# A gated convolution's result stored as two rounded parts, and loaded without a split ahead of its projection

## The chip, the core and the metric

The kernel runs on 1 core of one Trainium2 chip. The metric is device time in microseconds (us) of one execution. Three executions of the kernel before gave 1155.13 us (median), from 1154.42 to 1155.83.

Engines are named as in the profile: PE (TensorE matmuls; PEld its weight loads), DVE (VectorE), ACT (ScalarE), POOL (GpSimd), SP (SyncE, which here only issues DMAs; ACT issues some too).

## The reference, cut to what matters

An encoder layer over a sequence of 1024 rows and 1024 features, with two branches that read the same normalised input. One branch is a gated long convolution of width 512 ("hyena"), the other is attention with 8 heads. The change touches the result of the convolution, `zc` times its gate, between the convolution and the matmul with `w_hy_out`.

```python
h = rms_norm(x, g_norm[l])
proj = h @ w_in[l]
hy_in, z_hy, c_q, c_kv, k_rope, z_attn, gate_hy, gate_attn = jnp.split(proj, split_at, axis=-1)
u = short_conv(hy_in, w_short[l], b_short[l])
v_h, x1, x2 = jnp.split(u, 3, axis=-1)
zc = v_h
for o, gate in enumerate((x1, x2)):
    zc = gate * long_conv(zc, k_spec[:, o], hy_bias[l, o])
u_hy = (zc * jax.nn.silu(z_hy)) @ w_hy_out[l]
...
attn = dense_bidirectional_attention(q, k, v_a)
u_attn = (attn * jax.nn.silu(z_attn)) @ w_attn_out[l]
merged = g_hy * u_hy + g_at * u_attn
x = x + merged @ w_out[l]
```

## The kernel before, in words

Every f32 operand of a matmul is written as a sum of two rounded parts, high and low (type fp32r, names ending in h and l), and each product is made of three matmuls: high by high, high by low, low by high (`mm3`, L119, L121, L122). The helper `split` makes the parts: ACT casts the high part (L138), and DVE, or POOL where it is named, subtracts it for the low part (L139).

The stages in order of time. First the normalised input and the convolution's filters. Then the convolution in two halves, `convs(0)` and `convs(1)`, of two blocks of 128 features each (b = 0, 1 and b = 2, 3). Then `qkv`, which makes queries, keys and values (`pq`, `pkr`) and stores them to DRAM. Then what is left of the projections `pm` (L567) of the input onto the gate columns; these matmuls need nothing of the convolution and are strewn as filler between the stages from the filter on. Then attention: per head `pth` transposes queries and keys (L857), `S` holds the scores, `pr` the exponentials, `pt` their transposes (L901), `pv` the product with the values. Last comes the rest of the convolution branch, the projection of the attention branch, and the product with `w_out`.

**The result of the convolution.** At the end of `convs`, for each block b, a gate tile `gt` of 128x1024 is loaded from DRAM (L711), multiplied by the transposed convolution `pty` (L716, DVE), and stored to `yT[b]` in DRAM (L718). `gt` comes from a pool with one buffer, so the load for the next block waits until the tile of the block before is free.

**Its way back.** `hyena_load` (L986) loads the four `yT[b]` into tiles `yr` (L991) from a tag "gg" with three buffers, and splits each into `yh[i]` on ACT and `yl[i]` on POOL. `branch_out` (L963) then takes, for each of eight blocks d of the output columns, 256 KB of `w_hy_out` into a tile `wr` (L971), splits it into `wh` and `wl` (POOL while attention runs, DVE behind it), loads a gate tile `gg` (L976), and runs 24 matmuls `pmo` with the four `yh[i]` and `yl[i]`. Blocks d = 0, 1, 2 are written inside the pools of attention, as filler for PE; blocks 3 to 7 come behind attention.

**What sets the order.** The program text does not fix each engine's order. When the program is built, a list scheduler places all instructions on the engines by what is ready, and each engine then runs its list strictly in order. DMAs of SP are issued in the order of SP's list, onto one queue (q1); those of ACT onto another (q10). Near the start of attention, the queues' lists hold: the loads `qr`, `kr`, `vr` of the first pair of heads (L834), the `yr` loads, the `wr` loads of `w_hy_out`, the `gg` loads, and loads `z` (L935) for the attention's own gate. ACT's list holds there the casts `yh` and `wh`, and the pairs `ob` (L683), which read the projections `pm` out of PSUM; `pth` writes to PSUM space that the last `ob` has read.

Of the kernel before, what the change touches and what calls it, by code (L numbers as in the profile page):

```python
# [10 lines left out]
F32 = mybir.dt.float32  # L11
F32R = mybir.dt.float32r
# [7 lines left out]
P = 128  # L20
L = 1024
# [72 lines left out]
class K:  # L94
# [529 lines left out]
    def scratch(self):  # L624
        nc, a = self.nc, self.a
        dp = self.dp
        self.yT = [dp.tile([P, L], F32, tag=f"yT{i}", name=f"yT{i}") for i in range(4)]
        self.cT = [dp.tile([P, L], F32, tag=f"cT{i}", name=f"cT{i}") for i in range(6)]
        self.zaT = [dp.tile([P, L], F32, tag=f"zaT{i}", name=f"zaT{i}") for i in range(4)]
        self.gT = [dp.tile([P, L], F32, tag=f"gT{i}", name=f"gT{i}") for i in range(16)]  # L630
        self.g2, self.ud, self.xd = {}, {}, {}
# [61 lines left out]
    def convs(self, hf):  # L693
        nc = self.nc
        NB = CW // P
        uy = lambda nme: self.uq.tile([P, 8, CW], F32, tag="UY", bufs=2, name=self.nm(nme))
        U = uy("U")
        for g in range(2):
            nc.sync.dma_start(out=U[:, 4 * g:4 * g + 4], in_=self.ud[hf][g])
        Y = self.conv(0, hf, U)  # L700
        for g in range(2):
            xt = self.uq.tile([P, 4, CW], F32, tag="xt", name=self.nm("xt"))
            nc.sync.dma_start(out=xt, in_=self.xd[hf][g])
            nc.vector.tensor_tensor(out=Y[:, 4 * g:4 * g + 4], in0=Y[:, 4 * g:4 * g + 4], in1=xt, op=ALU.mult)
        for i in range(NB):
            self.xz(hf * NB + i)
        Y = self.conv(1, hf, Y)
        for i in range(NB):
            b = hf * NB + i
            gt = self.uq.tile([P, L], F32, tag="xt", name=self.nm("gt"))  # L710
            nc.sync.dma_start(out=gt, in_=self.g2[b])  # L711
            for g in range(2):
                ps = self.pp.tile([P, 4, P], F32, tag="cv", bufs=CVB, name=self.nm("pty"))
                for j in range(4):
                    nc.tensor.transpose(out=ps[:, j], in_=Y[:, 4 * g + j, i * P:(i + 1) * P], identity=self.ident)
                nc.vector.tensor_tensor(out=gt[:, g * 512:(g + 1) * 512], in0=gt[:, g * 512:(g + 1) * 512],  # L716
                                        in1=ps.rearrange("p a b -> p (a b)"), op=ALU.mult)
            nc.sync.dma_start(out=self.yT[b], in_=gt)  # L718


    def qkv(self, kp):
# [115 lines left out]
    def attention(self, wp, ssp, sp):  # L837

        nc, a = self.nc, self.a
# [111 lines left out]
        for u in range(64):  # L951
            h, qb = divmod(u, 8)
            if u + 1 < 64:
                scores(u + 1)
            trans(u)
            if u + 1 < 64:
                soft(u + 1)
            if u >= 2:
                pvs(u // 2 - 1, u % 2)
            if h + 1 < H and 2 <= qb < 6:  # L960
                prep(h + 1, qb - 2)
        pvs(31, 0)
# [19 lines left out]
                nc.vector.tensor_tensor(out=g[:, sl], in0=g[:, sl], in1=ps, op=ALU.mult)  # L982
                done(d, c, g[:, sl])

    def hyena_load(self, tp):
        nc = self.nc  # L986
        self.yh = [tp.tile([P, L], F32R, tag=f"yh{i}", name=f"yh{i}") for i in range(4)]
        self.yl = [tp.tile([P, L], F32R, tag=f"yl{i}", name=f"yl{i}") for i in range(4)]
        for i in range(4):
            y = tp.tile([P, L], F32, tag="gg", bufs=3, name=self.nm("yr"))  # L990
            nc.sync.dma_start(out=y, in_=self.yT[i])  # L991
            self.split(y, self.yh[i], self.yl[i], nc.gpsimd)
        self.m1 = {(d, c): self.dp.tile([P, 512], F32, tag=f"m1_{d}_{c}", name=f"m1_{d}_{c}") for d in range(8) for c in range(2)}

    def hyena_out(self, tp, pp, ds):
        def done(d, c, x):
# [155 lines left out]
@with_exitstack  # L1152
def hyena_mla_kernel(ctx, tc, a, out):
    k = K(ctx, tc, a, out)
    k.cp = ctx.enter_context(k.pool("cp"))
    k.dp = ctx.enter_context(k.pool("dp", space=DRAM))
    k.scratch()
    with k.pool("pp", space=PSUM) as k.pp:
        with ExitStack() as sr:
            hp = sr.enter_context(k.pool("hp", side="right"))  # L1160
            k.wp = sr.enter_context(k.pool("wp", side="right"))
            k.op = sr.enter_context(k.pool("op", side="right"))
            with k.pool("fp") as fp:
                with k.pool("xp") as xp, k.pool("fp1") as f1:
                    k.setup(xp)
                    k.load_x(xp, 0)
                    k.load_x(xp, 1)
                    k.filter_loads(f1)
                    k.build_hT(hp, xp)
                    k.filter_mlp(fp, f1)  # L1170
                    k.selection()
                svw = ExitStack()
                k.vw = svw.enter_context(k.pool("vw", side="right"))
                with k.pool("fpb") as fb:
                    k.filter_tables(fb)
                    with k.pool("fwk") as wk:
                        k.filter_spectra(wk)
                        for b in range(GEARLY):
                            k.fill_g(b)
            with k.pool("uq") as k.uq, k.pool("gp") as gp, k.pool("vb") as k.vb:  # L1180
                k.proj_vx(0)
                k.load_gu(gp)
                k.convs(0)
                k.proj_vx(1)
                k.convs(1)
            svw.close()
            for b in range(6):
                k.fill_c(b)
            with k.pool("kp") as kp:
                k.qkv(kp)  # L1190
            yp = ctx.enter_context(k.pool("yp"))
            srp = ExitStack()
            k.rp = srp.enter_context(k.pool("rp"))
            k.raw = {}
            k.load_pair(0)
            for b in range(4):
                k.fill_z(b)
            for b in range(GEARLY, 16):
                k.fill_g(b)
            k.hyena_load(yp)  # L1200
    with k.pool("gp2", side="right") as g2:
        k.ah = [g2.tile([P, L], F32R, tag=f"ah{i}", name=f"ah{i}") for i in range(4)]
        k.al = [g2.tile([P, L], F32R, tag=f"al{i}", name=f"al{i}") for i in range(4)]
        with k.pool("ssp", space=PSUM) as ssp, k.pool("asp", space=PSUM) as sp, k.pool("awp") as wp:
            k.mb = 1
            k.attention(wp, ssp, sp)
            k.hyena_out(yp, sp, range(HSPLIT))
        srp.close()
        with k.pool("tps", space=PSUM) as pp, k.pool("tlp") as tp:
            k.mb = 8  # L1210
            k.hyena_out(yp, pp, range(HSPLIT, 8))
            k.tail(yp, g2, tp, pp)
# [39 lines left out]
```

## Time and profile before

| | us |
|---|---|
| median of 3 executions | 1155.13 |
| lowest, highest | 1154.42, 1155.83 |
| the profiled execution | 1159.08 |
| its span in the profile | 1156.9 |
| PE busy | 1098.8 (95%) |
| DVE busy | 894.0 (77%) |
| ACT busy | 589.2 (51%) |
| POOL busy | 106.7 (9%) |

The profiled execution is one more execution than the three of the median, with its own time. The span is what the trace covers of it; the rest, 2.2 us, lies around it. Times of single instructions, as in the rows below, count from the start of the span. "Busy" adds up the time in which an engine executes something. The mean granted clock of PE was 0.984 of full speed.

### The profile page before, as it was taken

What the parts mean: (1) busy time and instruction counts of PE and PEld (TensorE: products, weight loads), DVE (VectorE), ACT (ScalarE), POOL (GpSimd) and SP (SyncE); (2) the same over time, 40 slices, a digit from 0 to 9 for tenths busy, and PEclk for the clock granted to TensorE, in tenths of its full rate; (3) what the DMA queues carried; (4) which work ended last, traced back from release to release, by engine and by line L of the source; (5) the groups of instructions that cost most, each with busy time, mean ns of one, the idle gap of its engine ahead of it and who ended that gap; (6) DMA issues with size and microseconds to landing.
All of it is one profiled execution on the core that took longest, in us unless ns stands there. A gap on an engine that the chain in (4) does not pass through costs nothing.

```text
span 1156.9 us, 15518 instructions
## 1 busy us (share of the span) xinstructions
PE 1098.8 (95%) x5525; PEld 912.7 (79%) x5525; DVE 894.0 (77%) x1631; ACT 589.2 (51%) x1097; POOL 106.7 (9%) x108
## 2 busy tenths in 40 slices
PE   4899999999999999999998999799999999999996
PEld 3678888888888888878887887688888888777875
DVE  6988788698788886778774793488888888678872
ACT  5735655754445434434424752687777777321420
POOL 0000000000000000000000132400000000232253
PEclk9989999999999999999999999899999999999999
DMA  5446454642335334334327558610202010886345
GB/s 211 132 146 194 153 166 175 204 119 64 88 90 142 110 110 131 91 90 125 91 82 226 153 152 284 201 56 12 90 1 92 1 65 1 265 272 208 90 129 182
DMA packets 119221, 150.27 MB, mean 130 GB/s; under 512 B 8548, under 2 KB 82408, under 8 KB 119144
## 3 DMA queue, kind: packets, MB, share of 16 engines
q1 hardware_dynamic: 107688, 120.97, 34.4%
q10 hardware_dynamic: 11456, 28.32, 6.5%
q8 instruction: 43, 0.70, 0.3%
q14 instruction: 34, 0.28, 0.1%
HBM read 101.81 MB, written 47.45 MB: 129 GB/s over the span
## 4 chain that ended last, share of the span: by engine, by line
PE 77%; DVE 8%; DMA 8%; ACT 4%; issue 2%; POOL 1%; SPq 0%; POOLq 0%; ACTq 0%; DVEq 0%
PE pm L567 35%; PE pu L128 8%; PE pt L901 5%; PE pi L128 4%; PE S L119 2%; PE S L121 2%; PE S L122 2%; PE pv L913 2%; PE pv L914 2%; PE po L122 2%; PE po L121 2%; PE po L119 2%; PE pmo L121 1%; PE pmo L119 1%; ACT pr L888 1%
## 5 line engine op out<-in xcount | busy, mean ns | idle before, releaser
L567 PE MATMUL pm<-hh,wh 128*128 128x512 f32 x656 | 208.8, 394 | 1.4 <-DVE hl L143 0.5
L567 PE MATMUL pm<-hl,wh 128*128 128x512 f32 x656 | 209.4, 394 | 0.0
L567 PE MATMUL pm<-hh,wl 128*128 128x512 f32 x656 | 208.3, 392 | 0.1
L567 PEld LDWEIGHTS pm<-hh,wh 128*128 128x128 f32 x656 | 123.1, 189 | 27.3 <-ACT wh L138 0.7
L567 PEld LDWEIGHTS pm<-hh,wl 128*128 128x128 f32 x656 | 123.4, 189 | 26.0 <-DVE wl L139 0.5
L567 PEld LDWEIGHTS pm<-hl,wh 128*128 128x128 f32 x656 | 123.5, 189 | 25.4
L138 ACT CAST wh<-wr 128x512 fp32r<-128x512 f32 x98 | 60.3, 621 | 152.0 <-PE pm L567 106.9
L138 ACT CAST PTh<-pt 128x512 fp32r<-128x512 f32 x128 | 72.8, 587 | 43.6 <-PE pt L901 41.8
L139 DVE TENSOR_TENSOR PTl<-pt,PTh 128x512 fp32r<-128x512 f32 x128 | 84.0, 683 | 14.0 <-ACT PTh L138 13.7
L886 DVE TENSOR_REDUCE mx<-S 128x1 f32<-128x1024 f32 x64 | 77.8, 1218 | 10.5 <-PE S L122 10.1
L139 DVE TENSOR_TENSOR wl<-wr,wh 128x512 fp32r<-128x512 f32 x95 | 66.2, 702 | 16.2 <-ACT wh L138 16.1
L901 PE MATMUL pt<-ident,pr 128*128 128x128 f32 x512 | 75.1, 276 | 1.1 <-ACT pr L888 0.2
L888 ACT ACTIVATE pr<-S,mx 128x1024 f32<-128x1024 f32 x64 | 71.7, 1121 | 5.4 <-DVE mx L886 5.1
L901 PEld LDWEIGHTS pt<-ident,pr 128*128 128x128 f32 x512 | 59.1, 140 | 15.5 <-ACT pr L888 2.9
L913 PE MATMUL pv<-PTh,vc 128*128 128x256 f32 x256 | 68.9, 297 | 0.0
L914 PE MATMUL pv<-PTl,vc 128*128 128x256 f32 x256 | 67.8, 293 | 0.0
L473 DVE TENSOR_TENSOR t<-pu,kt 128x512 f32<-128x512 f32 x64 | 41.0, 681 | 31.2 <-PE pu L128 30.5
L138 ACT CAST rh<-res 128x512 fp32r<-128x512 f32 x64 | 39.5, 619 | 42.8 <-PE pu L128 20.2
L119 PE MATMUL S<-kh,qh 96*128 96x512 f32 x128 | 53.0, 414 | 1.7 <-ACT pr L888 1.6
L121 PE MATMUL S<-kh,ql 96*128 96x512 f32 x128 | 52.5, 410 | 0.0
L913 PEld LDWEIGHTS pv<-PTh,vc 128*128 128x128 f32 x256 | 48.5, 189 | 4.4 <-DVE at L924 1.6
L122 PE MATMUL S<-kl,qh 96*128 96x512 f32 x128 | 50.8, 398 | 0.0
(285 smaller groups left out, 2402.2 us busy)
## 6 DMA issues: line engine op xcount, KB each, us to landing
wr<-in_w_in_dram SPq DMA_DIRECT2D x82, 256.0 KB, 3.2
wor<-in_w_out_dram SPq DMA_DIRECT2D x36, 256.0 KB, 4.6
dec<-in_dec_dram SPq DMA_DIRECT2D x16, 512.0 KB, 3.7
gT<-ob ACTq DMA_DIRECT2D x16, 512.0 KB, 3.3
gg<-gT SPq DMA_DIRECT2D x16, 512.0 KB, 3.9
kd<-kt ACTq DMA_DIRECT2D x28, 256.0 KB, 2.2
kt<-kd SPq DMA_DIRECT2D x28, 256.0 KB, 2.7
m<-gg ACTq DMA_DIRECT2D x16, 256.0 KB, 3.5
```

The lines of the kernel that those rows point to most:

```text
L119: m = nc.tensor.matmul(out, lhsT=lh, rhs=rh, start=start, stop=False)
L121: nc.tensor.matmul(out, lhsT=ll, rhs=rh, start=False, stop=False)
L122: nc.tensor.matmul(out, lhsT=lh, rhs=rl, start=False, stop=stop)
L128: m = self.nc.tensor.matmul(out, lhsT=x, rhs=y, start=n == 0, stop=n == len(ops) - 1)
L138: self.behind(self.nc.scalar.copy(out=hi, in_=x), after)
L139: (eng or self.nc.vector).tensor_tensor(out=lo, in0=x, in1=hi.bitcast(F32), op=ALU.subtract)
L567: nc.tensor.matmul(ps[c][0:m], lhsT=w[:, i, 0:m], rhs=h[d][:, c * 512:(c + 1) * 512], start=(d == 0 and f == 0), stop=(d == 7 and f == 2))
L886: nc.vector.tensor_reduce(out=mx, in_=ps, axis=AX.X, op=ALU.max, negate=True)
L888: nc.scalar.activation(out=pr, in_=ps, func=AF.Exp, bias=mx, accum_out=RS[h // 2][:, qb, h % 2:h % 2 + 1])
L901: nc.tensor.transpose(out=pt[:, i], in_=pr[:, kb * P:(kb + 1) * P], identity=self.ident)
L913: nc.tensor.matmul(pv, lhsT=V[h][:, kb], rhs=hi[:, kb], start=(kb == 0), stop=False)
L914: nc.tensor.matmul(pv, lhsT=V[h][:, kb], rhs=lo[:, kb], start=False, stop=(kb == 7))
```

## The change

`convs` splits each finished block into a high and a low part there, on ACT and DVE, and stores both: `yT[b]` becomes a pair of DRAM tiles. `hyena_load(i)` now loads block i's two parts from DRAM straight into `yh[i]` and `yl[i]`; the tiles `yr`, the four casts on ACT and the four subtracts on POOL are gone from that place. In the text of the program the call stands inside the loop of attention, at steps u = 8, 12, 16 and 20 of 64, and `hyena_tiles` only sets the tiles up.

```diff
@@ -624,7 +624,7 @@
     def scratch(self):
         nc, a = self.nc, self.a
         dp = self.dp
-        self.yT = [dp.tile([P, L], F32, tag=f"yT{i}", name=f"yT{i}") for i in range(4)]
+        self.yT = [[dp.tile([P, L], F32, tag=f"yT{x}{i}", name=f"yT{x}{i}") for x in "hl"] for i in range(4)]
         self.cT = [dp.tile([P, L], F32, tag=f"cT{i}", name=f"cT{i}") for i in range(6)]
         self.zaT = [dp.tile([P, L], F32, tag=f"zaT{i}", name=f"zaT{i}") for i in range(4)]
         self.gT = [dp.tile([P, L], F32, tag=f"gT{i}", name=f"gT{i}") for i in range(16)]
@@ -715,7 +715,10 @@
                     nc.tensor.transpose(out=ps[:, j], in_=Y[:, 4 * g + j, i * P:(i + 1) * P], identity=self.ident)
                 nc.vector.tensor_tensor(out=gt[:, g * 512:(g + 1) * 512], in0=gt[:, g * 512:(g + 1) * 512],
                                         in1=ps.rearrange("p a b -> p (a b)"), op=ALU.mult)
-            nc.sync.dma_start(out=self.yT[b], in_=gt)
+            y = [self.uq.tile([P, L], F32R, tag=f"y{x}", name=self.nm("y" + x)) for x in "hl"]
+            self.split(gt, *y)
+            for x in range(2):
+                nc.sync.dma_start(out=self.yT[b][x], in_=y[x].bitcast(F32))
 
 
     def qkv(self, kp):
@@ -957,6 +960,8 @@
                 soft(u + 1)
             if u >= 2:
                 pvs(u // 2 - 1, u % 2)
+            if u % 4 == 0 and 8 <= u < 24:
+                self.hyena_load(u // 4 - 2)
             if h + 1 < H and 2 <= qb < 6:
                 prep(h + 1, qb - 2)
         pvs(31, 0)
@@ -982,15 +987,14 @@
                 nc.vector.tensor_tensor(out=g[:, sl], in0=g[:, sl], in1=ps, op=ALU.mult)
                 done(d, c, g[:, sl])
 
-    def hyena_load(self, tp):
-        nc = self.nc
+    def hyena_tiles(self, tp):
         self.yh = [tp.tile([P, L], F32R, tag=f"yh{i}", name=f"yh{i}") for i in range(4)]
         self.yl = [tp.tile([P, L], F32R, tag=f"yl{i}", name=f"yl{i}") for i in range(4)]
-        for i in range(4):
-            y = tp.tile([P, L], F32, tag="gg", bufs=3, name=self.nm("yr"))
-            nc.sync.dma_start(out=y, in_=self.yT[i])
-            self.split(y, self.yh[i], self.yl[i], nc.gpsimd)
         self.m1 = {(d, c): self.dp.tile([P, 512], F32, tag=f"m1_{d}_{c}", name=f"m1_{d}_{c}") for d in range(8) for c in range(2)}
+
+    def hyena_load(self, i):
+        for x, t in enumerate((self.yh, self.yl)):
+            self.nc.sync.dma_start(out=t[i].bitcast(F32), in_=self.yT[i][x])
 
     def hyena_out(self, tp, pp, ds):
         def done(d, c, x):
@@ -1197,7 +1201,7 @@
                 k.fill_z(b)
             for b in range(GEARLY, 16):
                 k.fill_g(b)
-            k.hyena_load(yp)
+            k.hyena_tiles(yp)
     with k.pool("gp2", side="right") as g2:
         k.ah = [g2.tile([P, L], F32R, tag=f"ah{i}", name=f"ah{i}") for i in range(4)]
         k.al = [g2.tile([P, L], F32R, tag=f"al{i}", name=f"al{i}") for i in range(4)]
```

Since the scheduler sets each engine's order, three places show what moved. Line numbers behind the change are by 3 to 6 higher for the same statement. In the rows, x<-y is what is written and read.

SP's issues at the end of the convolution, between block b = 2 and the first loads of `wst` (weights of `qkv`), before:

```order
L718 DMA yT_62<-gt_5074 128x1024
L559 DMA wr_6996<-in_w_in_dram 128x4x128
L711 DMA gt_5089<-g_3_4660 128x1024
L718 DMA yT_63<-gt_5089 128x1024
L559 DMA wr_7032<-in_w_in_dram 128x4x128
L735 DMA wst_5522<-in_w_uq_dram 128x768
```

and with the change:

```order
L721 DMA yTh_64<-yh_5102 128x1024
L721 DMA yTl_65<-yl_5103 128x1024
L711 DMA gt_5108<-g_3_4674 128x1024
L559 DMA wr_7056<-in_w_in_dram 128x4x128
L721 DMA yTh_66<-yh_5122 128x1024
L721 DMA yTl_67<-yl_5123 128x1024
L559 DMA wr_7086<-in_w_in_dram 128x4x128
L738 DMA wst_5546<-in_w_uq_dram 128x768
```

Each block now has two stores in place of one, and the weight loads `wst` stand behind the second store of the last block, which is issued when DVE has made the low part.

SP's issues at the start of attention, before (three `yr` loads stand in a row, and two `wr` loads):

```order
L834 DMA qr_6356<-qd 128x1536
L834 DMA kr_6357<-kdr 128x1536
L834 DMA vr_6358<-vd 128x1024
L991 DMA yr_7170<-yT_60 128x1024
...
L971 DMA wr_9970<-in_w_hy_out_dram 128x4x128
...
L991 DMA yr_7182<-yT_63 128x1024
L976 DMA gg_9976<-gT_74 128x1024
```

and with the change:

```order
L837 DMA qr_6380<-qd 128x1536
L837 DMA kr_6381<-kdr 128x1536
L837 DMA vr_6382<-vd 128x1024
L997 DMA yh_7186<-yTh_60 128x1024
L997 DMA yl_7190<-yTl_61 128x1024
...
L997 DMA yh_7189<-yTh_66 128x1024
L997 DMA yl_7193<-yTl_67 128x1024
L938 DMA z_7998<-zaT_74 128x512
...
L976 DMA wr_9986<-in_w_hy_out_dram 128x4x128
...
L981 DMA gg_9992<-gT_78 128x1024
```

All eight loads of `yh` and `yl` stand in a row directly behind `vr`, not among the steps of attention; the first `wr` of `w_hy_out` stands behind them and behind two `z` loads.

ACT and PE at the start of attention. ACT before (the casts of `yr`, three and one, stand ahead of the last `ob` pair):

```order
L138 CAST yh_7162<-yr_7170 128x1024
...
L138 CAST yh_7164<-yr_7178 128x1024
L138 CAST wh_9972<-wr_9970 128x512
...
L138 CAST yh_7165<-yr_7182 128x1024
L683 ACTIVATE ob_7158<-pm_7096,cols 128x512
...
L684 DMA gT_89<-ob_7158 128x1024
...
L142 ACTIVATE qh_7228<-pth_7230,gq 96x512
...
L142 ACTIVATE kh_7244<-pth_7246,cols 96x512
...
L888 ACTIVATE pr_7273,rs_7270<-S_7263,mx_7271 128x1024
```

and with the change:

```order
L683 ACTIVATE ob_7182<-pm_7120,cols 128x512
...
L684 DMA gT_93<-ob_7182 128x1024
L142 ACTIVATE qh_7236<-pth_7238,gq 96x512
...
L142 ACTIVATE kh_7252<-pth_7254,cols 96x512
...
L138 CAST wh_9988<-wr_9986 128x512
...
L891 ACTIVATE pr_7281,rs_7278<-S_7271,mx_7279 128x1024
```

The last `ob` pair has no cast of a `yr` ahead of it, and the first `wh` stands behind `qh` and `kh`. PE's list at the same place, before (rows that continue a pattern left out):

```order
L567 MATMUL pm_7097<-hh_146,wl_7131 128x512
L857 MATMUL pth_7230<-ident,qr_6356 96x128 x4
L857 MATMUL pth_7237<-ident,qr_6356 96x128 x4
L119 MATMUL pmo_9978<-yh_7162,wh_9972 128x512
L121 MATMUL pmo_9978<-yh_7162,wl_9973 128x512
...
L857 MATMUL pth_7246<-ident,kr_6357 96x128 x4
...
L119 MATMUL S_7263<-kh_7244,qh_7228 128x512
```

and with the change:

```order
L567 MATMUL pm_7121<-hh_150,wl_7155 128x512
L860 MATMUL pth_7238<-ident,qr_6380 96x128 x4
L860 MATMUL pth_7245<-ident,qr_6380 96x128 x4
L860 MATMUL pth_7254<-ident,kr_6381 96x128 x4
...
L119 MATMUL S_7271<-kh_7252,qh_7236 128x512
...
L119 MATMUL pmo_9994<-yh_7186,wh_9988 128x512
L121 MATMUL pmo_9994<-yh_7186,wl_9989 128x512
```

Before, 28 `pmo` matmuls stand ahead of the first `pt` of attention, the first of them ahead of the transposes of `kr`. With the change 12 do, all in a row behind the scores `S`, and the `pt` stand behind them. Of the 192 matmuls `pmo` that read `yh` and `yl`, 120 stand behind attention before, and 156 with the change.

## Rows read from the trace of the kernel before

**Rows 1.** Three windows: PE, PEld, DVE, ACT, POOL busy us (instructions), PEclk, DMA share, GB/s

```profile
720.00:740.00 20.00, 12.09 (x53) 9.34 (x52) 4.38 (x6) 11.56 (x16) 16.34 (x11) 0.83 0.81 266
900.00:980.00 80.00, 79.84 (x532) 69.04 (x532) 68.69 (x97) 60.79 (x112) 2.90 (x3) 1.00 0.07 24
1010.00:1030.00 20.00, 20.00 (x88) 16.25 (x87) 9.94 (x16) 4.51 (x8) 5.16 (x4) 1.00 0.93 304
```

**Rows 2.** Waits of PE: us in total, times, longest us

```profile
PE ptx L230 <- DVE xs L223: 8.6, 1, 8.6
PE pth L857 <- ACT ob L683: 7.1, 1, 7.1
...
PE pq L119 <- ACT ch L142: 2.9, 1, 2.9
```

**Rows 3.** Timeline of PE, 715 to 745 us: start, us, work, [idle before <-releaser]

```profile
720.40 0.61 PE L567 MATMUL pm<-hh,wl 128*128 128x512 f32 x2
728.15 1.94 PE L857 MATMUL pth<-ident,qr 128*96 128x128 f32 x8 [7.13 <-ACT ob L683]
...
732.05 0.39 PE L119 MATMUL pmo<-yh,wh 128*128 128x512 f32 x1
732.28 0.39 PE L121 MATMUL pmo<-yh,wl 128*128 128x512 f32 x1
...
743.16 1.03 PE L901 MATMUL pt<-ident,pr 128*128 128x128 f32 x8
```

**Rows 4.** Timeline of ACT, 715 to 742 us

```profile
719.69 1.05 ACT L138 CAST yh<-yr 128x1024 fp32r<-128x1024 f32 x1 [8.47 <-DMA yr<-yT]
721.04 1.04 ACT L138 CAST yh<-yr 128x1024 fp32r<-128x1024 f32 x1 [0.30 <-DMA yr<-yT]
722.31 1.04 ACT L138 CAST yh<-yr 128x1024 fp32r<-128x1024 f32 x1 [0.23 <-DMA yr<-yT]
...
726.47 1.04 ACT L138 CAST yh<-yr 128x1024 fp32r<-128x1024 f32 x1 [2.00 <-DMA yr<-yT]
727.42 1.26 ACT L683 ACTIVATE ob<-pm,cols 128x512 f32<-128x512 f32 x2
...
733.38 0.62 ACT L138 CAST wh<-wr 128x512 fp32r<-128x512 f32 x1 [4.71 <-DMA wr<-in_w_hy_out_dram]
```

**Rows 5.** Timeline of SP's DMA issues, 600 to 740 us

```profile
618.42 0.34 SPq L718 DMA_DIRECT2D yT<-gt  x1
...
619.50 1.14 SPq L735 DMA_DIRECT2D wst<-in_w_uq_dram  x2
...
708.66 0.33 SPq L834 DMA_DIRECT2D qr<-qd  x1
...
723.20 0.34 SPq L991 DMA_DIRECT2D yr<-yT  x1
```

**Rows 6.** Timeline of POOL, 715 to 742 us

```profile
720.82 6.95 POOL L139 TENSOR_TENSOR yl<-yr,yh 128x1024 fp32r<-128x1024 f32 x3 [16.13 <-PE pm L567]
...
734.08 1.28 POOL L139 TENSOR_TENSOR wl<-wr,wh 128x512 fp32r<-128x512 f32 x1 [1.53 <-ACT wh L138]
```

**Rows 7.** Tile wst: a subtract of 128x1024 on DVE, min/median/max ns

```profile
L139 DVE TENSOR_TENSOR wkl<-wst,wkh x2: 1217/1222/1226, 634.2 to 640.6; 128x1024 fp32r<-128x1024 f32 x2
```

**Rows 8.** Timeline of DVE, 604 to 630 us

```profile
617.11 1.28 DVE L716 TENSOR_TENSOR gt<-gt,pty 128x512 f32<-128x512 f32 x2 [7.40 <-DMA gt<-g]
```

**Rows 9.** Timeline of PE, 604 to 646 us

```profile
627.84 0.62 PE L119 MATMUL pq<-wqh,ch 128*128 128x384 f32 x2 [2.94 <-ACT ch L142]
```

**Rows 10.** Timeline of PE, 1030 to 1046 us

```profile
1041.19 0.51 PE L119 MATMUL pmo<-ah,wh 128*128 128x512 f32 x1 [2.34 <-ACT wh L138]
1042.60 0.80 PE L121 MATMUL pmo<-ah,wl 128*128 128x512 f32 x1 [0.91 <-DVE wl L139]
...
1044.05 0.63 PE L121 MATMUL pmo<-ah,wl 128*128 128x512 f32 x1
1044.47 0.63 PE L122 MATMUL pmo<-al,wh 128*128 128x512 f32 x1
```

## The prediction, made before the changed kernel was run

> **What bounds the kernel now.** I read the page first: PE is busy 1098.8 of 1156.9 us, so a change can gain only where PE idles or where its clock falls. The table by windows shows where that is not: from 900 to 980 us, inside attention, PE is busy 79.84 of 80 us, and right behind attention, from 1010 to 1030, 20 of 20 [rows 1]. From 720 to 740 it is busy 12.09 of 20, at a granted clock of 0.83: attention starts there. The waits of PE, read next, name the place: the longest single wait after the kernel's first loads is 7.1 us, of `pth` for `ob` [rows 2].
>
> Then the timelines around it, one engine after the other. The last `pm` starts at 720.40, `pth` at 728.15 [rows 3]. `ob`, for which it waits, needs nothing but `pm`, but on ACT it stands behind the fourth cast of a `yr`: that cast starts at 726.47, `ob` at 727.42 [rows 4]. The cast waits for its load, which SP issued only at 723.20 [rows 5], as its buffer is one of three "gg" and came free when POOL had made the first `yl`, whose subtracts take 6.95 us for three, some 2.3 each, from 720.82 [rows 6]. So the chain is POOL, buffer, load, cast, `ob`, `pth`. The change removes it whole.
>
> **The change part by part.** The durations are those of one profiled execution, 1159.08 us long (span 1156.9 and 2.2 around it), 3.95 above the median of three, 1155.13; the sum is made against 1159.1 and then moved to the median.
>
> 1. The end of the convolution. Four casts of 1.04 us come to ACT [rows 4] and four subtracts of 1.22 to DVE, by one of the same shape [rows 7]. For blocks 0 to 2 nothing waits for them but stores, and PE has `pm` to run: 0 us. Without that cover a block would cost their 2.3 us.
>
> 2. The last block. Its product ends at 617.11 + 1.28 = 618.4 [rows 8], and `yT` goes out at 618.42, the `wst` loads behind it at 619.50 [rows 5]. Now cast and subtract (2.3) come between, and the cast stands behind other work on ACT, so `wst` comes 2.2 to 4.2 us later; I take 3.0. PE's list holds 22 more instructions, nearly all `pm`, ahead of the first `pq`, 22 x 0.23 = 5.0 us at the matmul pitch (732.05 to 732.28 in [rows 3]). PE idles 2.94 us there now [rows 9]; then 2.94 + 3.0 - 5.0 = 0.9. Five more `pm` lie inside the stage behind it (1.1 us), so the stage's end, its stores and the load `qr` come 3.0 to 4.1 later; with 3.5, `qr` is issued at 708.66 + 3.5 = 712.2 [rows 5]. No work is saved by this: those `pm` only come earlier.
>
> 3. The start of attention. `ob` no longer waits, so `pth` and `S` go right behind the last `pm`. But the scheduler put the eight y loads directly behind `vr`, and the first `wr` of `w_hy_out` behind these and two `z` loads; PE's list has twelve `pmo` between `S` and the first `pt`, and these need all eight tiles and the split `wr`. What is late next is therefore that `wr`, and behind the blocked `pmo` stand `pt`, and so all of attention. The casts of `yr` waited for their loads at 719.69, 721.04 and 722.31 [rows 4], so one 512 KB load lands each 1.31 us when the queue is full, and the first landed 719.69 - 708.66 = 11.0 us after `qr` was issued. With the change: first y part at 712.2 + 11.0 = 723.2, seven more 9.2, two `z` and one `wr` (768 KB, 1.5 x 1.31) 2.0: `wr` lands at 734.4. The cast takes 0.6 [rows 4] and the low part on POOL 1.3 [rows 6], which makes 736.3. Eleven more `pmo` take 2.5 us at the full pitch of 0.23, or 4.6 at 0.42, the pitch after an idle stretch (1044.05 to 1044.47 in [rows 10]); I take 3.6. The first `pt` starts at about 740.0, against 743.16 now [rows 3]. But before it now run 28 `pmo`, then only 12: the other 16 (3.7 us) are still to do. The fair comparison is 743.16 - 3.7 = 739.5, so **+0.5 us**: the old wait of 7.1 is nearly all given back to a new one. PE's smaller wait under 2 does not come on top, as the loads and not PE set this point. Bounds: `wst` late by 2.2 and full pitch give 738.1 (-1.4). If the queue moves only the 266 GB/s of the window from 720 to 740 [rows 1], a load takes 1.97 us, the 8.5 loads 5.6 us longer, and `pt` starts at 745.6 (+6.1). I stay near the 1.31, which is a row of this same queue with the same tiles.
>
> The rate of these loads, 512 KB in 1.31 us, is 400 GB/s [rows 4]. The Trainium skill, DMA: Bandwidth & Descriptors, section "Where 436 GB/s comes from", says instead that for transfers between HBM and SBUF the HBM side binds, at about 358 GB/s for a core. By that a load would take an estimated 1.46 us and the 8.5 loads 1.3 longer, and the sum below would be -0.4; the row speaks against it, and the measured rate is kept.
>
> 4. Inside attention PE is full [rows 1], so 20 more `pmo` that leave it make no loss by themselves; 36 in all go behind attention (156 there for 120). I put +0.3 (0 to 2) for gaps that they filled. The four POOL subtracts that are gone (9.4 us in all) were only in the chain above.
>
> 5. Behind attention. The 36 `pmo` add 8.3 us of PE work at the head of the last stage, in step with what was taken away above, so no time as such. But further on PE now waits 2.34 and 0.91 us for a weight's cast and subtract, and then runs seven matmuls 0.42 apart in place of 0.23, 1.4 us lost [rows 10]; ahead of that, DMA is busy 0.93 of the time [rows 1]. Eight more us of work ahead of it let loads and splits run ahead; their own loads and stores (some 1.3 MB, 4.3 us at 304 GB/s) take half of that back. Bounds: all of it goes (-4.6), or none, with a small loss (+1); I take half, **-2.5**.
>
> Sum: 0 + 0.5 + 0.3 - 2.5 = -1.7. Against 1159.1 that is 1157.4; against the median, **1153.4 us**.
>
> **The rivals.** A measurement of this kernel can tell about 0.2%, 2.3 us, from no change.
>
> *Forecast* (0.42): the wait changes its owner, the tail gives a little back: -4 to +0.9, mostly within 0.2%.
>
> *Clear gain* (0.23): `wst` is hardly later since DVE idles 7.40 us ahead of that product [rows 8], `pt` starts at 738.1, and the tail gives all: -1.4 + 0 - 4.6 = -6.0, 1149.1. For it: the 7.1 us that are removed are real. Against: the twelve `pmo` that stand ahead of `pt`.
>
> *Slower by the `wr` load* (0.22): eight loads of 512 KB on one queue hold up 256 KB of weights, for which PE stands still with attention behind it. At 266 GB/s `pt` starts at 745.6: +6.1 + 0.3 - 2.5 = +3.9, 1159.0; without the tail's gain +6.4, 1161.5. It decides when `wr` lands after 736.1, where item 3 costs what item 5 gains. For it: DMA is busy 0.81 in that window already [rows 1], and the y loads now move double the bytes, 4.2 MB. Against: the 1.31 us spacing.
>
> *No gain in the tail* (0.13): its waits are set by DMA, whose traffic moves along with the 36 matmuls. Then 0.5 + 0.3 = +0.8, 1155.9; with `wst` 5 us late, +3.
>
> **How the numbers follow.** Faster by over 0.2%: 0.15 of the forecast's 0.42, all of the gain's 0.23, 0.02 of the rest: 0.40. Within: 0.24 + 0.02 + 0.07 = 0.33. Slower: 0.03 + 0.19 + 0.05 = 0.27. The likeliest case alone has the range 1151.1 to 1156.0. The range for 8 in 10 takes in the gain's 1149.1 with 2.1 below it, as the profiled times and the medians spread, and the slower case up to 1161.0: 1147.0 to 1161.0.
>
> **What would show it.** Right, step by step: the wait of `pth` for `ob` is gone, `pth` starts within 2 us of the last `pm`; SP issues `qr` near 712, `wr` lands near 734, PE's new longest wait in mid-kernel is of a `pmo` for `wh` (5 us or more), the first `pt` starts near 740; PE's wait before the first `pq` falls to about 1; the waits at 1041 shrink. Wrong: `pt` after 743, which means that the loads take longer than 1.31 each or that the convolution's end is later than 3 us; `pt` before 738, which means that `wr` does not wait for the y loads; a new wait of PE inside attention; or a tail with the same waits as now.

## The result: 1169.59 us for 1155.48, slower

| | before | changed |
|---|---|---|
| median, us | 1155.48 (4 runs) | 1169.59 (4 runs) |
| lowest, highest | 1154.42, 1156.40 | 1168.50, 1170.27 |
| the profiled execution, its span | 1159.08, 1156.9 | 1170.25, 1168.5 |
| PE, DVE, ACT, POOL busy | 1098.8, 894.0, 589.2, 106.7 | 1102.1, 897.1, 588.1, 97.7 |

The ratio is 1.0122, 95% interval 1.0104 to 1.0139: 14 us slower, outside the range that was given (1147 to 1161). The kernel before was profiled once more later (1157.21 us, span 1155.1); both of its traces are used below, since the first execution, 1159.08, lies 3.6 us over the median of its runs.

**The profile after.** The waits of PE, as [rows 2] (engine, line, what for; us in total, times, longest):

```profile
PE pmo L119 <- ACT wh L138: 9.0, 3, 7.5
...
PE pq L119 <- ACT q L797: 2.9, 1, 2.9
PE ptt L611 <- DVE acc L600: 2.9, 1, 2.9
...
PE pmo L121 <- DVE wl L139: 2.6, 2, 1.7
...
PE pth L860 <- ACT ob L683: 0.6, 1, 0.6
```

The wait of `pth` for `ob`, 7.1 us, is gone as forecast. In its place stands one of 7.5 us of the first `pmo` for `wh`. New is also an early one, of `ptt`, the transposes of a short convolution near 230 us: 2.9 us, where the kernel before has

```profile
PE ptt L611 <- DVE acc L600: 0.7, 2, 0.5
```

PE's timeline at the start of attention, as [rows 3]:

```profile
721.28 1.08 PE L860 MATMUL pth<-ident,qr 128*96 128x128 f32 x8 [0.55 <-ACT ob L683]
...
725.87 0.80 PE L119 MATMUL S<-kh,qh 96*128 96x512 f32 x1 [0.77 <-ACT kh L142]
726.46 0.63 PE L121 MATMUL S<-kh,ql 96*128 96x512 f32 x1
726.89 0.63 PE L122 MATMUL S<-kl,qh 96*128 96x512 f32 x1
...
730.73 0.63 PE L122 MATMUL S<-kl,qh 96*128 96x512 f32 x1
738.90 0.80 PE L119 MATMUL pmo<-yh,wh 128*128 128x512 f32 x1 [7.54 <-ACT wh L138]
740.24 0.79 PE L121 MATMUL pmo<-yh,wl 128*128 128x512 f32 x1 [0.55 <-POOL wl L139]
...
745.10 1.61 PE L904 MATMUL pt<-ident,pr 128*128 128x128 f32 x8
```

`S` starts 4.6 us behind `pth`, the twelve `pmo` stand still until 738.90, and the first `pt` comes at 745.10. The twelve `S` and, behind the wait, the twelve `pmo` run 0.43 apart once they are under way, where 0.23 is the full pitch. ACT's timeline there, as [rows 4]:

```profile
725.14 1.25 ACT L142 ACTIVATE kh<-pth,cols 96x512 fp32r<-96x512 f32 x2
738.23 0.62 ACT L138 CAST wh<-wr 128x512 fp32r<-128x512 f32 x1 [11.84 <-DMA wr<-in_w_hy_out_dram]
738.86 1.28 ACT L891 ACT_TABLE_LOAD   x1
740.16 1.11 ACT L891 ACTIVATE pr<-S,mx 128x1024 f32<-128x1024 f32 x1
```

ACT is done with `kh` at 726.4 and then waits 11.84 us, in order, for the `wr` of `w_hy_out`. Behind that cast stand the table load and the first exponential `pr`, whose scores were done at 731.4. So PE, from 731.4 on, and ACT, from 726.4 on, both stand still for one 256 KB load. SP's issues, as [rows 5] (start, length, what):

```profile
613.41 0.47 SPq L721 DMA_DIRECT2D yTl<-yl  x1
...
624.22 0.32 SPq L721 DMA_DIRECT2D yTl<-yl  x1
...
625.30 1.90 SPq L738 DMA_DIRECT2D wst<-in_w_uq_dram  x2
...
716.49 0.33 SPq L837 DMA_DIRECT2D qr<-qd  x1
...
717.83 0.67 SPq L997 DMA_DIRECT2D yh<-yTh  x1
...
731.17 0.38 SPq L976 DMA_DIRECT2D wr<-in_w_hy_out_dram  x1
```

`wst` goes out 5.8 us later than before, `qr` 7.8 us later. The last block's product, in DVE's timeline as [rows 8], ends 3.4 us later than before, at 621.8:

```profile
620.52 1.28 DVE L716 TENSOR_TENSOR gt<-gt,pty 128x512 f32<-128x512 f32 x2 [3.15 <-DMA gt<-g]
```

From `qr` to the cast of `wr` it is 738.23 - 716.49 = 21.7 us; 22.2 were forecast. The windows, as [rows 1]:

```profile
720.00:740.00 20.00, 9.37 (x33) 5.90 (x31) 5.26 (x6) 6.58 (x10) 3.58 (x3) 0.64 1.02 396
900.00:980.00 80.00, 78.70 (x521) 67.20 (x520) 67.28 (x92) 60.39 (x110) 2.80 (x3) 1.00 0.02 8
```

While the y loads run, DMA is busy throughout (1.02) and moves 396 GB/s. PE's granted clock is 0.64 in this window, an average over its two levels, full and half: it fell to half near 726, behind the gaps between `pm`, `pth` and `S`, and stayed there over the wait of the `pmo`.

**Where the 14 us lie.** The table takes start times of certain matmuls in PE's timelines, and counts what was moved across them. "Again" is the second trace of the kernel before. The last two columns are changed minus before (first trace, second trace), after 0.2275 us, the full pitch, has been taken off for each `pm` or `pmo` more, or added for each fewer (`pi`: the convolution's first inverse transform; `pkv`: the last product of `qkv`).

| stretch | before | again | changed | matmuls more | by trace 1 | by trace 2 |
|---|---|---|---|---|---|---|
| start to first `pi` | 244.91 | 245.41 | 247.06 | 0 | +2.2 | +1.7 |
| to first `pq` | 382.93 | 381.37 | 386.56 | 22 | -1.4 | +0.2 |
| to the last `pkv` or `pq` | 58.76 | 56.59 | 58.80 | 5 | -1.1 | +1.1 |
| to the first `pt` | 56.56 | 58.72 | 52.68 | -43 | +5.9 | +3.7 |
| to the last `S` (attention) | 234.18 | 234.20 | 234.36 | -15 | +3.6 | +3.6 |
| to the last `pmo` of `yh` | 38.09 | 38.12 | 47.10 | 31 | +2.0 | +1.9 |
| to the last matmul | 131.64 | 131.90 | 130.11 | 0 | -1.5 | -1.8 |
| to the end | 9.84 | 8.75 | 11.79 | 0 | +1.9 | +3.0 |
| sum | 1156.9 | 1155.1 | 1168.5 | 0 | +11.6 | +13.4 |

A single row is not sharper than some 2 to 3 us. The two traces of the kernel before differ by 2.2 us from `qkv` on, and in six traces in which PE's list up to the first `pq` is that of the kernel before (these two and runs 3, 7, 10 and 11 below) the first row lies between 242.9 and 246.0. The last two rows belong together: they sum to 141.5 and 140.6 before and to 141.9 in the changed kernel.

### The profile page after: what moved, and what is told of

Its sections match the earlier page's. It is cut to its first block, busy times and chain, and to the rows that moved or that the text cites. A ratio compares the mean times of both kernels' runs of the same rounds, so it can differ in the third digit from the quotient of the medians.

```text
span 1168.5 us, 15540 instructions
## 1 busy us (share of the span) xinstructions
PE 1102.1 (94%) x5525; PEld 912.5 (78%) x5525; DVE 897.1 (77%) x1635; ACT 588.1 (50%) x1097; POOL 97.7 (8%) x104
## 4 chain that ended last, share of the span: by engine, by line
PE 69%; DMA 11%; DVE 11%; ACT 5%; issue 2%; POOL 1%; SPq 1%; ACTq 0%; POOLq 0%; DVEq 0%
PE pm L567 33%; PE pu L128 8%; PE pt L904 5%; PE pi L128 4%; DMA wor<-in_w_out_dram 3%; PE S L119 2%; PE pv L916 2%; PE S L121 2%; PE S L122 2%; PE pv L917 2%; ACT pr L891 2%; PE pmo L121 1%; PE pmo L122 1%; PE pmo L119 1%; DMA yl<-yTl 1%
```

## The experiments

The kernels of one group ran on one chip beside the kernel before, whose medians were 1155.8 (1 to 4), 1157.3 (5 to 8), 1156.4 (9 to 11) and 1157.7 (12). Every ratio is to that, with its 95% interval; medians of different groups are compared less sharply than ratios.

**1. Room alone.** The early wait of `ptt` lies 200 us ahead of anything that the diff edits. Of the diff, only the added tiles could reach that far; here they come alone:

```diff
+            y = [self.uq.tile([P, L], F32R, tag=f"y{x}", name=self.nm("y" + x)) for x in "hl"]
             nc.sync.dma_start(out=self.yT[b], in_=gt)
```

> The kernel before, with the two extra 128x1024 tiles of the convolution's pool set up but never used. In the trace of the changed kernel PE waits 2.9 us for the last step of an early short convolution (ptt for acc) where the kernel before waits 0.7, and SP issues the two loads gur there behind the stores u. Theory A (the room that the two tiles take in the pool moves a neighbour's place, and its loads must wait longer): about 1157.5 us, 2 over before, with the wait of ptt near 2.9. Theory B (that wait comes of the changed order of the matmuls, or is chance): 1155.5, wait 0.7.

Measured: 1159.56 (10 runs, 1155.3 to 1161.8), ratio 1.0026 (1.0011 to 1.0042), about 3 us; `ptt` waits 3.3.

```profile
PE pth L858 <- ACT ob L683: 9.2, 1, 9.2
...
PE ptt L611 <- DVE acc L600: 3.3, 1, 3.3
```

The tile `gur` shows the path (first and last start at the end of a line). In the kernel before:

```profile
L621 SPq DMA_DIRECT2D gur<-in_gu_dram x2: 371/414/457, 185.7 to 186.2; - x2
L138 ACT CAST guh<-gur x2: 1371/1374/1377, 217.4 to 218.7; 128x1408 fp32r<-128x1408 f32 x2
```

and in the changed kernel:

```profile
L621 SPq DMA_DIRECT2D gur<-in_gu_dram x2: 568/1050/1532, 211.0 to 212.3; - x2
L138 ACT CAST guh<-gur x2: 1370/1373/1376, 218.5 to 221.6; 128x1408 fp32r<-128x1408 f32 x2
```

SP issues the two loads at 186 before, and at 211 in the changed kernel and in this one, among two stores `u`. The casts of `guh` come up to 2.9 us later, and DVE's subtracts `gul`, which stand ahead of the step `acc` that `ptt` needs, with them. Tiles that are never used cost 3 us, with PE's list that of the kernel before from first to last: theory A holds. The other traces agree. In the seven with the two tiles (the changed kernel, 1, 2, 4, 5, 9 and 12) `gur` goes out at 210.1 to 212.6 us, `ptt` waits 2.7 to 3.4 us and the first `pi` starts at 246.1 to 248.9; in the seven without (both of the kernel before, 3, 6, 7, 10 and 11) `gur` goes out at 183.9 to 186.3 us, `ptt` waits at most 0.9 us at once and `pi` starts at 242.8 to 246.0. That the neighbour's place became free later was concluded from this order, not seen.

**2. The split and the two stores alone**, the way back as before:

```diff
+            y = [self.uq.tile([P, L], F32R, tag=f"y{x}", name=self.nm("y" + x)) for x in "hl"]
+            self.split(gt, *y)
             nc.sync.dma_start(out=self.yT[b], in_=gt)
+            nc.sync.dma_start(out=self.yL[b], in_=y[1].bitcast(F32))
```

> The kernel before, with the split at the end of the convolution and two stores per block (the product and its low part), while the way back is as before: yr loads, casts on ACT, subtracts on POOL. PE's list at the start of attention is that of before. Theory A (the convolution's end costs little but the room; the loss lies at the start of attention and behind it): 1157 to 1159 us. Theory B (the late weight loads behind the second store set the loss): 1162 or more, with a PE wait before the first pq over 4 us.

Measured: 1164.46 (1162.2 to 1165.6), ratio 1.0068 (1.0046 to 1.0091). The size is theory B's; the sign that it named is not in the trace: PE waits 2.7 us ahead of the first `pq`, as before, and not over 4.

```profile
PE pth L861 <- ACT ob L684: 11.8, 1, 11.8
...
PE ptt L611 <- DVE acc L600: 2.8, 1, 2.8
PE pq L119 <- ACT ch L142: 2.7, 1, 2.7
```

The wait of `pth` for `ob` grew to 11.8 us where 1 has 9.2. PE's list has 17 more `pm` ahead of the first `pq` and 15 fewer behind `qkv` (135); yet from the last matmul of `qkv` to `pth` it takes 42.8 us, as with 150 of them (43.6 in 1, 41.6 and 43.1 before). There the chain of stores, loads and casts sets the time, so a `pm` that is taken from there saves nothing, while ahead of `pq` it comes on top (386.5 us from the first `pi` to the first `pq`, for 383.0 in 1). The median lies 4.9 us above that of 1, which has the tiles too. In the traces `pq` comes 2.1 and the first `pt` 4.4 us later than in 1. The split, the second store and the moved `pm` came together here, so that the `pm` account for this is read from the traces, not tested alone.

**3. The loads alone.** The change, but with one store per block at the end of `convs`; both tiles of a block are loaded from it, so the low part is left out and the output is another:

```diff
-            nc.sync.dma_start(out=self.yT[b], in_=gt)
...
+            self.nc.sync.dma_start(out=t[i].bitcast(F32), in_=self.yT[i])
```

> The change without its part at the convolution's end: one store per block, and both tiles of a block are loaded from the same stored product, unsplit (the low part is left out of the computation, so the output is another). Ten pmo stand ahead of the transposes of kr here, and three wh casts on ACT ahead of the first exponential. Theory A (the loads cost because weights of w_hy_out queue behind them, and PE and ACT stand still for these): qr near 708.7, the first wh cast near 729.5, the first pt near 744 to 747, total 1157 to 1161. Theory B (the loads are free, the convolution's end costs): 1150 to 1154.

Measured: 1162.12 (1160.3 to 1165.3), ratio 1.0052 (1.0033 to 1.0072), slower as theory A has it, though over its 1157 to 1161. The signs in the trace came earlier than I gave: `qr` at 704.6 and not 708.7, the first cast of a `wr` at 726.1 and not 729.5, the first `pt` at 740.4 and not 744 to 747 (the first `pq` is at 624.8). The new wait is there without any split in the convolution:

```profile
PE pmo L119 <- ACT wh L138: 11.1, 2, 10.4
```

Parts 2 and 3 cost 8 and 6 us alone, as much together as the whole change costs. The trace of 3 is of its fastest execution (1160.34), so it shows less than the 6.

**4. Only `pmo` held.** In the changed kernel the first matmul of each `pmo` group gets an order edge to a transposition of step 4 of attention; nothing waits at run time for that edge, it only places the group in the list.

```diff
+                             after=self.hold if self.mb == 1 and b == 0 else None)
```

> The changed kernel with its first pmo held back in PE's list to behind step 4 of attention; ACT's list still has the cast of the first wr ahead of the first exponential. Theory A (ACT is blocked too: the exponentials cannot start before the wr has landed): the first wh cast stays near 738, pt starts near 741.5, total 1166 to 1169, little better than 1169.6. Theory B (only the twelve pmo block attention): pt near 734, total near 1161.

Measured: 1165.24, ratio 1.0080 (1.0055 to 1.0104), 4.4 under the changed kernel and just under theory A's 1166 to 1169; first `pt` at 741.04. ACT's timeline:

```profile
724.65 1.25 ACT L142 ACTIVATE kh<-pth,cols 96x512 fp32r<-96x512 f32 x2
737.86 0.62 ACT L138 CAST wh<-wr 128x512 fp32r<-128x512 f32 x1 [11.95 <-DMA wr<-in_w_hy_out_dram]
738.49 1.28 ACT L891 ACT_TABLE_LOAD   x1
739.78 1.11 ACT L891 ACTIVATE pr<-S,mx 128x1024 f32<-128x1024 f32 x1
```

ACT alone stops attention: it waits 11.95 us for `wr`, and `pt` now waits 10.2 us for `pr`. Theory A holds.

**5. `pmo` and the casts of `wr` held.**

```diff
-            self.split(r, wh, wl, nc.gpsimd if self.mb == 1 else nc.vector)
+            self.split(r, wh, wl, nc.gpsimd if self.mb == 1 else nc.vector, after=self.hold if self.mb == 1 else None)
```

> The changed kernel with both the first pmo on PE and the casts of wr on ACT held back to behind step 4 of attention, so that neither list has anything that waits for a wr ahead of the first exponential; all else, the y loads and the 123 pm between the last matmul of the stage qkv and attention among it, is as in the changed kernel. Theory A (the loss at the start is ACT and PE standing still in order for wr): the first pt near 733.5 where it was 741.0 with pmo alone held, total 1157 to 1160. Theory B (the queue of 4.2 MB itself slows the start, whoever waits): pt 738 or later, total 1163 or more.

Measured: 1156.78 (10 runs, 1151.6 to 1158.4), ratio 0.9994 (0.9979 to 1.0008), just under theory A's 1157 to 1160; first `pt` at 730.37, where 733.5 was forecast. It is 12.8 us under the changed kernel by the medians and 14.8 by the ratios, and 8.5 to 9.9 under 4, the worth of ACT's block alone. ACT's timeline, and PE's first `pt`:

```profile
724.15 1.25 ACT L142 ACTIVATE kh<-pth,cols 96x512 fp32r<-96x512 f32 x2
725.42 1.28 ACT L891 ACT_TABLE_LOAD   x1
729.11 1.11 ACT L891 ACTIVATE pr<-S,mx 128x1024 f32<-128x1024 f32 x1 [2.40 <-DVE mx L889]
...
730.37 1.66 PE L904 MATMUL pt<-ident,pr 128*128 128x128 f32 x8
```

The table load follows `kh` at once. The same 4.2 MB are loaded in the same place, at 375 to 422 GB/s from 724 to 740, and nothing ahead of `pt` waits for them: theory A holds, and the full queue as such is not the price.

Not all of the gain lies at the start, though. Between the two traces, 15.0 us apart, 13.7 lie between the last matmul of `qkv` and the first `pt`. Behind that, attention is 1.3 and the stretch to the last `pmo` of `yh` 3.8 us longer (twelve more `pmo` stand there, 2.7 us), and from there to the end it is 5.3 shorter.

**6. The change without added room**, the two parts in a buffer that the pool has:

```diff
-            y = [self.uq.tile([P, L], F32R, tag=f"y{x}", name=self.nm("y" + x)) for x in "hl"]
+            y = self.uq.tile([P, 2, L], F32R, tag="UY", bufs=2, name=self.nm("yy"))
+            y = [y[:, x] for x in range(2)]
```

> The changed kernel with the two parts of a block in a buffer that the pool has already, so no added room. The scheduler's list then has gur ahead as in the kernel before and nothing waiting for wr ahead of the first pt, but 1893 pm ahead of the first pq (1831 before, 1853 changed) and only 91 behind qkv (150 and 123). Theory A (a pm that is pulled ahead delays the chain from qkv to the loads qr, and is missing as cover behind it): the early wait of ptt falls to 0.7, the first pq starts near 640, PE idles some 6 us ahead of pth, pt near 738.5, total 1161 to 1165. Theory B (only the room and the lists at the start of attention count): total 1154 to 1158.

Measured: 1158.82 (1157.1 to 1162.2), ratio 1.0019 (1.0006 to 1.0032), between the two theories. The wait of `ptt` is gone (0.2), and the cover, the `pm` that PE could do while it waits, is gone too:

```profile
PE pth L861 <- DMA qr<-qd: 6.8, 1, 6.8
```

But `pt` came at 731.3, not 738.5: I had added the 62 early `pm` in full to the start of `pq`, which came at 637.8 and not 640, and the stages behind it took less than I gave them. This run has nothing ahead of `pt` that waits for `wr`, like 5, and so it does not separate the room by itself.

**7. The kernel before with the same holds** (its `yr` casts too, and all behind step 2), and **8. the kernel before again**, without an edit:

```diff
-            self.split(y, self.yh[i], self.yl[i], nc.gpsimd)
+            self.split(y, self.yh[i], self.yl[i], nc.gpsimd, after=self.hold)
```

> The kernel before, with its yr casts, the casts of wr and the first pmo held back to behind step 2 of attention; the store, the yr loads and the POOL subtracts are those of before. Theory A (what the start of attention lost before was ACT and PE waiting in order, which needs no split at the convolution's end to be mended): pth within 1 us of the last pm, the first pt near 733, total 1150 to 1154. Theory B (the loads and splits merely move into attention and are paid there): 1156 or more.

Measured: 1158.56, ratio 1.0013 (0.9997 to 1.0029), no gain: my theory A fell, theory B holds. The start went as forecast, even better (first `pt` at 724.9), and all was paid back: attention took 239.8 us for 234.2, and 27 more `pmo` stood behind it (147 for 120).

> The kernel before once more, unchanged, for a second trace: how far each stage differs between two executions. The wait of pth for ob 7 us within 1, the first pt within 1 us of the first trace's once the time of the first pq is taken off, the early wait of ptt 0.7.

Measured: 1157.21; the wait for `ob` 8.7 and not within 1 of 7.1; the first `pt` at 742.1, which is 115.3 us behind the first `pq`, as in the first trace; the wait of `ptt` 0.9 at the longest. How far the stretches differ stands below the table.

**9 to 11. Filler written into the steps of attention.** With the holds of 7, now in both kernels, `branch_out` yields after each group of three matmuls, and the loop of attention takes one group in every second step:

```diff
+            if u == 5:
+                self.fill = self.hyena_out(self.yp, sp, range(HSPLIT))
+            if u >= 5 and (u * 1) % 2 < 1:
+                next(self.fill, None)
```

> The changed kernel with the casts of wr and the first pmo held to behind step 2 of attention, and the 72 pmo of the blocks d = 0 to 2 written into the steps of attention, three in every second step from step 5 on, so that all 72 stand inside attention (24 where only held, and 144 of the 168 behind it move to 120). Theory A (attention takes some 235 us from its first pt to its last score whatever PE does beside it, so a pmo inside is free and one behind it costs its 0.227 us): that stretch stays within 2 us of 235.7, 48 matmuls leave the stretch behind attention (40 us there to 29), total 1145 to 1149 against 1156.8 when only held. Theory B (PE is the bound of attention, its busy share being 99%): the stretch grows by the 11 us, total 1155 to 1158.

Measured: 1157.55, ratio 1.0008 (0.9999 to 1.0017), no better than 5 and far from theory A's 1145 to 1149. Attention took 245.2 us where 5 has 235.7: 49 `pmo` more (11.1 us) made it 9.5 longer. Theory A fell, theory B holds.

> The same on the kernel before: store, yr loads and POOL subtracts of before, its yr casts, wr casts and pmo held to behind step 2, and the 72 pmo written into the steps. Theory A: the first pt near 725 as when only held, attention near 236 to 240, total 1143 to 1148; and less than the changed kernel treated alike by what the change costs ahead of attention (room 3 us, pm pulled ahead 2 to 5). Theory B: 1156 to 1159, as when only held.

Measured: 1154.94 (1150.4 to 1159.4), ratio 0.9983 (0.9965 to 1.0001); first `pt` at 730.2 and not near 725, attention 248.4 us and not 236 to 240. Theory A fell here too, and the median lies just under theory B's range as well. Treated alike, the kernel before is 2.6 us under the changed one (10 against 9; the intervals just touch).

For the last one, four blocks in place of three, a group is taken in three of five steps:

```diff
-HSPLIT = 3
+HSPLIT = 4
```

> As the run before, with the 96 pmo of four blocks written into attention, three in three of five steps. Theory A as long as the bubbles of attention hold them (some 19 us are lost there by PE with 48 pmo inside, room for 80 more): 3 to 6 us under the run with three blocks. Theory B (the bubbles are used up, or buffers of gg and wr wait): no gain, or a longer attention.

Measured: **1153.21** (1150.1 to 1155.5), ratio 0.9965 (0.9953 to 0.9978): 4 us under the kernel before. Theory A wanted it 3 to 6 us under 10; it is 1.7 under, and the runs of 10 spread over 9, so a gain of the fourth block is not shown. Attention took 251.1 us with 96 `pmo`, 2.7 more than in 10 for 24 matmuls (5.5 us).

**12. The first `wr` ahead of the y loads**, in the changed kernel:

```diff
+        for d in range(1):
+            r = tp.tile([P, 4, P], F32, tag="wr", bufs=2, name=self.nm("wr"))
...
+            self.pre["w_hy_out", d] = r
...
+            r = self.pre.pop((nme, d), None)
```

> The changed kernel with the load of the first wr of w_hy_out issued ahead of the eight y loads; nothing else is edited. PE's list then has eleven pmo between the transposes of qr and those of kr, and the cast of this wr stands ahead of the last ob pair on ACT. Theory A (anything in PE's list ahead of the first pt that needs the y loads stops attention until they have landed, 1.3 us each): pmo follow the y loads as they land, the second transposes of kr start near 736, the first pt near 744, total 1166 to 1171. Theory B (the place of wr behind 4.2 MB is the price): pt near 735, total 1158 to 1162.

Measured: 1168.59, ratio 1.0109 (1.0077 to 1.0141), as slow as the change; `kr`'s second transposes at 736.15, first `pt` at 743.63, all as theory A has it. PE's timeline:

```profile
729.79 0.49 PE L122 MATMUL pmo<-yl,wh 128*128 128x512 f32 x1 [0.34 <-DMA yl<-yTl]
731.99 0.52 PE L119 MATMUL pmo<-yh,wh 128*128 128x512 f32 x1 [1.70 <-DMA yh<-yTh]
...
733.85 0.80 PE L122 MATMUL pmo<-yl,wh 128*128 128x512 f32 x1 [0.92 <-DMA yl<-yTl]
...
736.15 1.05 PE L860 MATMUL pth<-ident,kr 128*96 128x128 f32 x4
...
743.63 1.04 PE L904 MATMUL pt<-ident,pr 128*128 128x128 f32 x8
```

Now each `pmo` waits for its y tile. The place of `wr` in the queue is not the price; what counts is that instructions which need the loads stand, in order, ahead of those that do not.

## Why the prediction was wrong

It forecast -1.7, and each of its terms was too low. By the table, and the prediction's items (numbers in brackets are the experiments):

- **Item 1, forecast 0, measured +2 to +3.** "Nothing waits for them but stores" looked at time and left out room. Two tiles that nobody waits for moved a load 25 us back in another stage (1).
- **Items 2 and 3, forecast +0.5 up to the first `pt`, measured +3.4 and +5.0.** Item 3 had the right wait, at the right length: 21.7 us from `qr` to the cast, 22.2 by its sum. But `qr` started 4.3 us later than item 2 had it. Of the 5.8 us by which `wst` was late, for which 3.0 were taken, the split is 2.4 (product to `wst`: 3.5 us for 1.1) and was well judged; 2.2 is the late start of the whole convolution, item 1's room; 1.2 came in the convolution, where five more `pm` stood ahead of the last product. From `wst` to `qr` came 2.0 more where 0.5 were taken (the two traces of the kernel before differ by 1.5 there). Then the eleven `pmo` ran 0.43 apart throughout, not halfway between that and 0.23, which is 1 us more. Item 2's "no work is saved by this: those `pm` only come earlier" put no price on the places that they left: where a load chain sets the time, time does not shrink with the `pm` (2).
- **Item 3, the second list.** It looked at PE's list alone: "behind the blocked `pmo` stand `pt`". On ACT the cast of that `wr` stands ahead of the first exponential, in rows that the order of ACT shows; that alone puts `pt` at 741.0 (4). Taking both blocks away is worth 13 to 15 us (5), the largest single effect here. That is more than the 3.4 to 5.0 of the row above, as the kernel before had a loss of its own there, the wait for `ob`: the changed kernel lost that one and got a longer one.
- **Item 4, forecast +0.3, measured +3.6.** "Inside attention PE is full" was read from 79.84 of 80 us. That row does not say it: a record of a matmul is 0.39 long and the next starts 0.23 later, so idle time up to 0.16 at each does not show. The Trainium skill, Perfetto Trace Analysis, section "Identifying the Most-Contended Engine", calls the busy time of matmuls no good measure of how near PE is to its limit, as they are pipelined, and goes by the busy time of weight loads instead. The trace agrees: the weight loads of the same row [rows 1] are busy 69.04 of 80. Attention took 234.2 us with 38 `pmo` and 234.4 with 23; it holds for 1, 2, 3 and 12 too (233.9 to 234.4, 22 or 38 inside). So 15 `pmo` had been free in there, and were then paid for behind. Not all would be: 49 more by hand cost 9.5 of their 11.1 us (9). What sets attention's 234 us was not looked for.
- **Item 5, forecast -2.5, measured +2.4 and +3.1.** Its waits did not shrink in sum. Between 1030 and 1050 they are 4.1 us in the changed kernel, 3.6 and 2.4 in the two traces before:

```profile
1038.96 0.50 PE L119 MATMUL pmo<-ah,wh 128*128 128x512 f32 x1 [0.81 <-ACT wh L138]
1040.36 0.50 PE L121 MATMUL pmo<-ah,wl 128*128 128x512 f32 x1 [0.91 <-DVE wl L139]
...
1046.63 0.49 PE L119 MATMUL pmo<-ah,wh 128*128 128x512 f32 x1 [0.64 <-ACT wh L138]
...
1048.83 0.50 PE L121 MATMUL pmo<-ah,wl 128*128 128x512 f32 x1 [1.70 <-DVE wl L139]
```

Ahead of that, the stretch to the last `pmo` of `yh` is 2 us longer. Two waits of `pmo` for `gg` lie there, 1.06 us at 993 and 0.78 at 997; in the kernel before the two lay ahead of the first `pt`:

```profile
734.36 0.50 PE L119 MATMUL pmo<-yh,wh 128*128 128x512 f32 x1 [0.78 <-DVE gg L982]
742.12 0.50 PE L119 MATMUL pmo<-yh,wh 128*128 128x512 f32 x1 [0.97 <-DVE gg L982]
```

The rest, from the last `pmo` of `yh` to the end, is 0.4 and 1.3 us longer (141.9 for 141.5 and 140.6), and 1 and 2, with 120 `pmo` behind attention as before, have 140.8 and 141.8: no loss is shown there. The gain that item 5 hoped for does occur, but elsewhere: in 4, 5 and 6, with 168 `pmo` behind attention, this stretch takes 134.8 to 136.6. Why it comes with 168 and not with 156 stays open.

The rival "slower by the `wr` load", at 0.22, had the sign and PE's wait, but priced it by a slower queue, 1159 to 1161.5. The queue was not slow: 396 GB/s from 720 to 740 is the prediction's 400. Nor is the place of `wr` in it the price (12), and the rival had nothing of what items 1 and 4 measured. The Trainium skill, DMA: Bandwidth & Descriptors, section "Where 436 GB/s comes from", has the HBM side bind transfers between HBM and SBUF at about 358; the measurement decides against it here.

## What to carry to other kernels

Where a scheduler fills an engine with spare work, that work is a stock: what a change makes late draws on it, and it is then missing where a chain of loads needs cover, so count it stretch by stretch in both orders. Before a moved load, read every in-order list for the first instruction that needs it and for what stands behind that, ACT's as well as PE's: order edges that put two of them back were worth 13 to 15 us with the same transfers, of which 13.7 lay at that place in the traces. A new tile also takes room, and a busy share near 100% made of overlapped records does not prove that an engine is the bound; the same stretch with another amount of its work tells.

## What was not expected of the hardware

PE's granted clock fell to its lower level, 0.50, near 726 in the changed kernel, after three gaps of 0.55, 1.45 and 0.77 us between `pm`, `pth` and `S`, and was back at 1.00 only near 746, behind the twelve `pmo`. An estimate from the two pitches, 0.43 and 0.23: the 24 scores and `pmo` between took 24 x 0.2 = 4.8 us more than at the full pitch. In run 5 it fell there too, but with `pt` and more scores close behind the first scores it was back from 732.
